# Norms between the layers: all tiles at once with scale and shift per feature, or tile by tile with a row scale and a shift added in PSUM

## Chip, cores, metric

One core of a Trainium2 chip runs the whole program in one launch. The metric is the device time of one execution in microseconds (us); the numbers are the median of three runs.

## The reference, cut to what matters

Two blocks of two layers each over 512 tokens of width 1024. The first block is a gated linear attention layer (GLA) and a dilated attention layer, each with memory attention; the second has a joint attention layer with a mixture of experts, then a neighbourhood attention layer with a second mixture. Each layer reads a normed residual:

```python
def rmsnorm(x, w):
    return (x * lax.rsqrt(jnp.mean(x * x, axis=-1, keepdims=True) + EPS)) * w
def modulate(x, g, shift, scale):
    return rmsnorm_2(x, g) * (1 + scale) + shift
# first block
for i in range(2):
    h = rmsnorm(x, norm_w[i])
    branch = mixer_i(h)                       # GLA, then dilated; gated
    x = x + branch @ w_out[i]
x = rmsnorm(x, final_norm_w)
# second block
for l in range(2):
    h_l = modulate(x_lat, norm_mix[l], sh1, sc1)
    h_c = modulate(x_ctx, norm_mix[l], sh1c, sc1c)
    o_c, o_l = mixer_l(h_c, h_l)              # joint attention, then neighbourhood
    x_lat = x_lat + g1 * o_l
    ...                                       # mixture of experts, adds to x_lat (and x_ctx)
```

Shift and scale are vectors over the 1024 features, computed in the program from the conditioning input.

## The kernel before, in words

The 512 tokens stand as four tiles of 128 rows x 1024 features (`K.tok`, tile `xres`); a layer's products want them with features on the partitions, as eight blocks of 128 features x 512 tokens, split into a high and a low part (`hh`, `hl`) whose three products make one float32 product (`mm3`, L256: lines 259 to 261).

**The norm.** `norm_T` (L367) takes all tiles of a set: it scales each by its reciprocal root (L377 on VectorE for odd tiles, L379 on ScalarE for even ones), transposes every 128x128 block on TensorE (L386) into one bank per feature block, and evacuates the bank. Without a shift, ScalarE writes the high part with the feature's scale (L390) and VectorE the low part (L391). With a shift, scale and shift go into a tile `nt` first, on ScalarE or VectorE in turn, and `split` (L137) makes the high part by a copy on ScalarE (L139) and the low part by a subtraction (L140), on VectorE or, for blocks 1 and 3, on GpSimd.

**Three places.** (G) The end of `gla_layer`, L793 to L808, before the dilated layer: no shift, and `phase_order` reorders tokens. (D) The end of `dil_layer`, L1100 to L1137, before the joint layer: latent norm with shift, composed with the first block's final norm (row `fw`), beside a norm of two context tiles. (N) `na_norms` (L2327), after the first mixture: the latent norm `lat()`, then `ctx()`, which adds the mixture to the two context tiles (`add_ctx`, L2194) and norms them.

**Order.** At G and D the norm is woven with the output product (`out_steps`, L683). `weave` (L24) advances several generators by estimated cost and due time (`yield cost, delay`); it sets the order in which each engine's instructions are written, and each engine runs its own in order. The output product makes 1024 columns in four parts of 256: two by `tm`, the last two together by `tm2` (L307), which finishes token tile after tile. `Residual.add` (L822) adds each part to the residual and collects sums of squares; `complete(tiles)` lets the norm go on. Before the change the norm asks for all four tiles. Between the product's own work VectorE and ScalarE also split the next weights (`cut`, L188: L208 and L211) and VectorE sums the conditioning product (L1396).

At N, `run(lat)` writes the whole latent norm first; then `weave(ctx, bg=(proj,))` writes the context part beside the next layer's projection, whose first context tile waits for the flag `nactx`. In `add_ctx` small placeholder DMAs on the SP queue (L2199, L2202) read `after`, which is `K.scaled`, a corner of the last scaled tile of the norm before; the rows are then fetched and added.

`features` (L355) brings vectors of 1024 into columns by a DMA each and one transpose. `na_mod` (L2316) does this for N; it is called inside `moe_layer` (L2294), between the routing table and the loop over overflow blocks.

Of the kernel before, what the change touches and what calls it, by code (L numbers as in the profile page):

```python
# [8 lines left out]
F32 = mybir.dt.float32  # L9
# [64 lines left out]
class Core:  # L74
# [289 lines left out]
        self.nc.vector.tensor_copy(t, ps[:, :n])  # L364
        return t

    def norm_T(self, pool, rows, rstd, hi, lo, sc, sh=None, tag="t", dst=None, src=lambda x: x):  # L367


        nc = self.nc  # L370
        n = len(rows)
        w = n * 128
        ys = []
        for i, x in enumerate(rows):
            y = pool.tile([128, D], F32, name=f"y{i}")
            if i % 2:
                nc.vector.tensor_scalar(y, x, rstd[i], None, op0=OP.mult)  # L377
            else:
                nc.scalar.activation(y, x, AF.Copy, scale=rstd[i])  # L379
            ys.append(y)  # L380
        self.scaled = ys[-1][0:1, 0:1]
        yield 0, 1500
        for k in range(8):
            ps = self.ps(tag)
            for i, y in enumerate(ys):
                nc.tensor.transpose(ps[:, i * 128:(i + 1) * 128], y[:, k * 128:(k + 1) * 128], self.ident)  # L386
            h, l = (dst(x[:, k, :]) if dst else x[:, k, :w] for x in (hi, lo))
            s = sc[:, k:k + 1]
            if sh is None:
                nc.scalar.activation(h, src(ps[:, :w]), AF.Copy, scale=s)  # L390
                nc.vector.scalar_tensor_tensor(l, src(ps[:, :w]), s, h.bitcast(F32), op0=OP.mult, op1=OP.subtract)  # L391
            else:
                t = pool.tile([128, w], F32, name="nt", bufs=3)
                if k % 2:
                    nc.scalar.activation(t, ps[:, :w], AF.Identity, scale=s, bias=sh[:, k:k + 1])
                else:
                    nc.vector.tensor_scalar(t, ps[:, :w], s, sh[:, k:k + 1], op0=OP.mult, op1=OP.add)
                self.split(h, l, src(t), nc.gpsimd if k in (1, 3) else None)
            yield n * 109, 0

    def bcast_row(self, pool, name, src, n=D, eng=None, **kw):

# [288 lines left out]
def gla_layer(K, A):  # L691
# [101 lines left out]
    K.dhh = ph.tile([128, 8, T], F32R, name="dhh")  # L793
    K.dhl = ph.tile([128, 8, T], F32R, name="dhl")
    with K.pool("gE", side="right") as st:
        nw = K.features(st, "nw1", [A["norm_w1"].rearrange("o (k p) -> (o k) p", p=128)])
        for i in range(4):
            nc.gpsimd.dma_start(xr[:, i, :], xin[i])
        r = Residual(K, st, K.tok, "gla", spill=[K.xbuf[i] for i in range(4)])

        def norms():
            yield from r.complete(range(4))
            rs = K.rsqrt(r.sum(range(4)), 4, 1.0 / D)
            yield 0, 2500
            yield from K.norm_T(st, K.tok, [rs[:, i:i + 1] for i in range(4)], K.dhh, K.dhl, nw,
                                dst=phases, src=phase_order)
        weave(norms(), out_steps(K, range(4), tokens(bh, bl), r.add))
    K.close(gC)  # L808
    K.close(gA)
# [223 lines left out]
def dil_layer(K, A):  # L1033
# [64 lines left out]
    with K.pool("dE") as st:  # L1098
        for i in range(4):
            nc.gpsimd.dma_start(xr[:, i, :], K.xbuf[i])  # L1100
        K.psum(p=(2, 512), t=(4, 512))
        fw = K.bcast_row(st, "fw", A["final_norm_w"], eng=nc.sync)
        r = Residual(K, st, K.tok, "dil", row=fw)
        vec = lambda ap: ap.rearrange("(k p) -> k p", p=128)
        m = K.features(st, "mv", [vec(K.mods[0, s, o * D:(o + 1) * D]) for s in range(2) for o in range(2)]
                       + [vec(A["norm_mix_2"][0]), vec(A["final_norm_w"])])
        sh, sc = [m[:, 0:8], m[:, 16:24]], [m[:, 8:16], m[:, 24:32]]
        for s in range(2):
            nc.vector.scalar_tensor_tensor(sc[s], sc[s], 1.0, m[:, 32:40], op0=OP.add, op1=OP.mult)
        nc.vector.tensor_tensor(sc[0], sc[0], m[:, 40:48], op=OP.mult)  # L1110
        tok = lambda k, tt: tuple(x[:, tt * 128:(tt + 1) * 128] for x in blocks(k))

        def ctx_norm():
            x = []
            for i in range(2):
                x.append(st.tile([128, D], F32, name=f"cx{i}"))
                nc.sync.dma_start(x[i], A["ctx_2"][i * 128:(i + 1) * 128, :])

            rs = K.row_rstd(x, K.hc[0].rearrange("p a b -> p (a b)")[:, :D])
            yield 0, 3000  # L1120
            yield from K.norm_T(st, x, [rs[:, i:i + 1] for i in range(2)], *K.hc, sc[1], sh[1])

        def norms():

            yield from r.complete(range(4))
            s1, s2 = r.sum(range(4)), r.sum(range(4), r.sw)
            u = K.small.tile([128, 4], F32, name="u")
            nc.vector.tensor_scalar(u, s1, EPS, EPS * EPS * D, op0=OP.mult, op1=OP.add)
            nc.vector.tensor_tensor(u, u, s2, op=OP.add)
            rs = K.rsqrt(u, 4, 1.0 / D, 0.0)  # L1130
            yield 0, 2500
            if K.stop != "b1":
                yield from K.norm_T(st, K.tok, [rs[:, i:i + 1] for i in range(4)], hh, hl, sc[0], sh[0])
            rs = K.rsqrt(s1, 4, 1.0 / D)
            for t in range(4):
                nc.vector.scalar_tensor_tensor(K.tok[t], K.tok[t], rs[:, t:t + 1], fw, op0=OP.mult, op1=OP.mult)
        weave(ctx_norm(), norms(), out_steps(K, range(4), tok, r.add))  # L1137
# [1175 lines left out]

def na_mod(K, A, p):  # L2316

    vec = lambda ap: ap.rearrange("(k p) -> k p", p=128)
    m = K.features(p, "mv", [vec(K.mods[1, s, o * D:(o + 1) * D]) for s in range(2) for o in range(2)]
                   + [vec(A["norm_mix_2"][1])], "h")  # L2320
    sh, sc = [m[:, 0:8], m[:, 16:24]], [m[:, 8:16], m[:, 24:32]]
    for s in range(2):
        K.nc.vector.scalar_tensor_tensor(sc[s], sc[s], 1.0, m[:, 32:40], op0=OP.add, op1=OP.mult)
    return sh, sc


def na_norms(K, hh, hl, p, cx, ss, mod):  # L2327


    nc = K.nc  # L2330
    sh, sc = mod

    def lat():
        rs = K.rsqrt(ss[:, 0:4], 4, 1.0 / D)
        yield from K.norm_T(p, K.tok, [rs[:, i:i + 1] for i in range(4)], hh, hl, sc[0], sh[0],
                            dst=lambda x: x[:, 64:576].rearrange("p (c r) -> p r c", r=8),
                            src=lambda t: t.rearrange("p (r c) -> p r c", c=64))
        nc.scalar.activation(hh[:, :, 0:64], hh[:, :, 512:576].bitcast(F32), AF.Copy)
        nc.scalar.activation(hl[:, :, 0:64], hl[:, :, 512:576].bitcast(F32), AF.Copy)

    def ctx():
        K.moe.add_ctx(p, cx, ss, K.scaled)
        yield 0, 9000
        rs = K.rsqrt(ss[:, 4:6], 2, 1.0 / D)
        yield from K.norm_T(p, cx, [rs[:, i:i + 1] for i in range(2)], hh[:, :, 576:], hl[:, :, 576:], sc[1], sh[1])
        K.set("nactx")
    return lat(), ctx()

# [151 lines left out]
def tile_two_blocks(ctx: ExitStack, tc: tile.TileContext, A, out, stop=None):  # L2500
# [27 lines left out]
    cx = [x2[:, i, :] for i in range(2)]  # L2528
    ss = p.tile([128, 6], F32, name="ss")
    mod = []  # L2530
    moe_layer(K, K.moe, K.tok, ss, lambda: mod.append(na_mod(K, A, p)))
    if stop == "moe0":
        return store()

# [146 lines left out]
```

## Time and profile before

| | |
|---|---|
| median of three runs | 3170.08 us (3168.34 to 3170.78) |
| the profiled execution's own time | 3168.85 us |
| its span, first to last instruction | 3167.1 us |
| mean granted TensorE clock | 0.961 |
| busy: PE / PEld / DVE / ACT / POOL | 92 / 77 / 72 / 57 / 18 % of the span |
| chain that ended last, by engine | PE 18 %, DVE 1 % |

PE is TensorE's products, PEld its weight loads (beside them), DVE VectorE, ACT ScalarE, POOL GpSimd, SP the queue that issues most transfers. A timeline row gives start, duration, engine, line, operation, output<-inputs and tile shape; in square brackets stands how long the engine idled before it and what ended that. A window row gives the busy time of each engine with its number of instructions, then the clock and the DMA share.

### The profile page before, as it was taken

What the parts mean: (1) busy time and instruction counts of PE and PEld (TensorE: products, weight loads), DVE (VectorE), ACT (ScalarE), POOL (GpSimd) and SP (SyncE); (2) the same over time, 40 slices, a digit from 0 to 9 for tenths busy, and PEclk for the clock granted to TensorE, in tenths of its full rate; (3) what the DMA queues carried; (4) which work ended last, traced back from release to release, by engine and by line L of the source; (5) the groups of instructions that cost most, each with busy time, mean ns of one, the idle gap of its engine ahead of it and who ended that gap; (6) DMA issues with size and microseconds to landing.
All of it is one profiled execution on the core that took longest, in us unless ns stands there. A gap on an engine that the chain in (4) does not pass through costs nothing. (4 is left out here: it accounts for less than half of the span.)

```text
span 3167.1 us, 46620 instructions
## 1 busy us (share of the span) xinstructions
PE 2906.3 (92%) x17395; PEld 2429.5 (77%) x17395; DVE 2264.8 (72%) x3684; ACT 1792.8 (57%) x2961; POOL 568.2 (18%) x871
## 2 busy tenths in 40 slices
PE   7989899999889889996999999959998789999997
PEld 6858688888779777785888888748887678888885
DVE  4776666765556566657898898875545688888888
ACT  4543534343352466534888788854334368878885
POOL 2110142523232111022111111020001211111110
PEclk9989999999989899997999999979999889999998
DMA  6334433433431200034999999954334399999996
GB/s 210 127 114 135 146 120 121 147 134 133 154 122 29 77 28 1 1 110 173 364 378 372 342 362 365 354 171 142 101 100 143 116 327 366 352 332 348 355 365 202
DMA packets 146089, 636.31 MB, mean 201 GB/s; under 512 B 30787, under 2 KB 37283, under 8 KB 86850
## 3 DMA queue, kind: packets, MB, share of 16 engines
q1 hardware_dynamic: 104034, 568.56, 49.6%
q0 software_dynamic: 29664, 50.29, 5.0%
q10 hardware_dynamic: 12160, 14.43, 1.9%
q8 instruction: 139, 2.28, 0.3%
q14 instruction: 92, 0.75, 0.1%
HBM read 615.13 MB, written 48.58 MB: 210 GB/s over the span
## 5 line engine op out<-in xcount | busy, mean ns | idle before, releaser
L211 DVE TENSOR_TENSOR wlo<-wraw,whi 128x1024 fp32r<-128x1024 f32 (+1 forms) x936 | 1105.6, 1222 | 251.4 <-ACT whi L208 239.2
L208 ACT ACTIVATE whi<-wraw 128x1024 fp32r<-128x1024 f32 (+1 forms) x938 | 935.9, 1051 | 184.7 <-PE ps_p L260 54.2
L260 PE MATMUL ps_h<-wlo,xth 128*128 128x512 f32 x1024 | 416.1, 406 | 1.3 <-DVE wlo L211 1.1
L259 PE MATMUL ps_h<-whi,xth 128*128 128x512 f32 x1024 | 409.5, 400 | 2.9 <-ACT xth L139 2.9
L261 PE MATMUL ps_h<-whi,xtl 128*128 128x512 f32 x1024 | 405.2, 396 | 0.0
L259 PE MATMUL ps_p<-whi,dhh 128*128 128x256 f32 (+3 forms) x828 | 248.5, 301 | 10.4 <-ACT qa L1541 6.4
L260 PE MATMUL ps_p<-wlo,dhh 128*128 128x256 f32 (+3 forms) x828 | 240.5, 291 | 0.0
L261 PE MATMUL ps_p<-whi,dhl 128*128 128x256 f32 (+3 forms) x828 | 239.5, 290 | 0.0
L259 PEld LDWEIGHTS ps_h<-whi,xth 128*128 128x128 f32 x1024 | 194.1, 190 | 48.3 <-ACT xth L139 4.0
L260 PEld LDWEIGHTS ps_h<-wlo,xth 128*128 128x128 f32 x1024 | 194.0, 189 | 47.5 <-DVE wlo L211 6.3
L261 PEld LDWEIGHTS ps_h<-whi,xtl 128*128 128x128 f32 x1024 | 193.7, 189 | 40.1
L259 PE MATMUL ps_y<-whi,hth 128*128 128x512 f32 x512 | 205.5, 401 | 5.8 <-DVE xg L2156 2.9
L1396 DVE SCALAR_TENSOR_TENSOR acc<-wraw,cs,acc 128x512 f32<-128x512 f32 x280 | 203.2, 759 | 9.7 <-DMA wraw<-in_w_ada_dram 8.1
L260 PE MATMUL ps_y<-wlo,hth 128*128 128x512 f32 x512 | 203.2, 397 | 0.2
L261 PE MATMUL ps_y<-whi,htl 128*128 128x512 f32 x512 | 202.5, 395 | 0.0
L2213 POOL DMA_INDIRECT xg<-hbuf,idx x64 | 86.5, 1351 | 545.3 <-PE ps_x L2224 480.8
L259 PEld LDWEIGHTS ps_p<-whi,dhh 128*128 128x128 f32 x828 | 157.7, 191 | 25.5 <-ACT qa L1541 6.6
L260 PEld LDWEIGHTS ps_p<-wlo,dhh 128*128 128x128 f32 x828 | 158.1, 191 | 1.3
L261 PEld LDWEIGHTS ps_p<-whi,dhl 128*128 128x128 f32 x828 | 157.7, 191 | 1.3
L2290 POOL DMA_INDIRECT ybuf<-y,idx x62 | 66.1, 1067 | 469.3 <-ACT y L2286 434.8
L139 ACT ACTIVATE xth<-ps_x 128x512 fp32r<-128x512 f32 x128 | 75.5, 590 | 76.4 <-PE ps_h L260 40.8
L259 PEld LDWEIGHTS ps_y<-whi,hth 128*128 128x128 f32 x512 | 96.7, 189 | 27.9 <-ACT whi L208 3.3
(792 smaller groups left out, 6716.4 us busy)
## 6 DMA issues: line engine op xcount, KB each, us to landing
wraw<-in_moe_w_gate_dram SPq DMA_DIRECT2D x128, 1024.0 KB
wraw<-in_moe_w_up_dram SPq DMA_DIRECT2D x128, 1024.0 KB
wraw<-in_moe_w_down_dram SPq DMA_DIRECT2D x128, 1024.0 KB
wraw<-in_w_ada_dram SPq DMA_DIRECT2D x48, 1024.0 KB
wraw<-in_db_w_dram SPq DMA_DIRECT2D x27, 1024.0 KB
wraw<-in_w_out_dram SPq DMA_DIRECT2D x8, 1024.0 KB
wraw<-in_na_qk_dram SPq DMA_DIRECT2D x8, 1024.0 KB
ntab<-in_na_tab_dram SPq DMA_DIRECT2D x16, 384.0 KB
```

Source lines behind the costliest of these rows:

```text
L139: nc.scalar.activation(hi, src, AF.Copy)
L208: self.nc.scalar.activation(h, x, AF.Copy)
L211: (self.cut_eng or self.nc.vector).tensor_tensor(l, x, h.bitcast(F32), op=OP.subtract)
L259: mm(out, ah, bh, start=first, stop=False)
L260: mm(out, ah, bl, start=False, stop=False)
L261: mm(out, al, bh, start=False, stop=last)
L1396: nc.vector.scalar_tensor_tensor(acc[s], x, w, acc[s], op0=OP.mult, op1=OP.add)
L2213: self.K.nc.gpsimd.indirect_dma_start(out=xg, out_offset=None, in_=self.hbuf, in_offset=bass.IndirectOffsetOnAxis(ap=gi, axis=0), bounds_c ...
L2290: self.K.nc.gpsimd.indirect_dma_start(out=self.ybuf, out_offset=bass.IndirectOffsetOnAxis(ap=si, axis=0), in_=y, in_offset=None, bounds_ch ...
```

## The change

`norm_tile` takes one tile: one VectorE instruction scales by the reciprocal root and by a broadcast row of feature scales; four blocks of 128 features go through TensorE into one bank of 512 columns (a transpose, or, with a shift, a float32 product with the identity and a one-row product of the shift with ones, which adds the shift in PSUM); ScalarE copies the bank and VectorE subtracts. At G and D tiles 0 and 1 are normed once `complete((0, 1))` holds, then 2, then 3; at N all four in a row. The scaled tiles take turns in two buffers `yt`. `scale_row` and `shift_row` fetch the rows; the latent vectors leave `features`.

```diff
--- before.py
+++ after.py
@@ -364,7 +364,7 @@
 
-    def norm_T(self, pool, rows, rstd, hi, lo, sc, sh=None, tag="t", dst=None, src=lambda x: x):
+    def norm_T(self, pool, rows, rstd, hi, lo, sc, sh=None, tag="t", dst=None, src=lambda x: x, ring=False):
 
@@ -372,7 +372,7 @@
         for i, x in enumerate(rows):
-            y = pool.tile([128, D], F32, name=f"y{i}")
+            y = pool.tile([128, D], F32, name="yt", bufs=2) if ring else pool.tile([128, D], F32, name=f"y{i}")
             if i % 2:
@@ -397,6 +397,47 @@
             yield n * 109, 0
+    def norm_tile(self, pool, x, rstd, row, shift, put, view=lambda v: v, tag="t"):
+        nc = self.nc
+        y = pool.tile([128, D], F32, name="yt", bufs=2)
+        nc.vector.scalar_tensor_tensor(y, x, rstd, row, op0=OP.mult, op1=OP.mult)
+        self.scaled = y[0:1, 0:1]
+        yield 0, 1500
+        for b in range(2):
+            ps = self.ps(tag)
+            for j in range(4):
+                k = slice((4 * b + j) * 128, (4 * b + j + 1) * 128)
+                o = ps[:, j * 128:(j + 1) * 128]
+                if shift is None:
+                    nc.tensor.transpose(o, y[:, k], self.ident)
+                else:
+                    nc.tensor.matmul(o, y[:, k], self.ident, start=True, stop=False)
+                    nc.tensor.matmul(o, shift[0][:, k], shift[1], start=False, stop=True)
+            h, l = put(b)
+            v = view(ps.rearrange("p (k t) -> p k t", k=4))
+            nc.scalar.activation(h, v, AF.Copy)
+            nc.vector.tensor_tensor(l, v, h.bitcast(F32), op=OP.subtract)
+            yield 870, 0
+    def scale_row(self, pool, l, side, w, t=None):
+        sc = pool.tile([128, D], F32, name="scrow")
+        if t is None:
+            t = pool.tile([128, D], F32, name="yt", bufs=2)
+        self.bcast(t, w)
+        self.bcast(sc, self.mods[l, side, D:2 * D])
+        self.nc.vector.scalar_tensor_tensor(sc, sc, 1.0, t, op0=OP.add, op1=OP.mult)
+        return sc
+    def shift_row(self, pool, l, side):
+        sh, one = pool.tile([1, D], F32, name="shrow"), pool.tile([1, 128], F32, name="one")
+        self.nc.gpsimd.memset(one, 1.0)
+        self.nc.sync.dma_start(sh, self.mods[l, side, 0:D].rearrange("(o n) -> o n", o=1))
+        return sh, one
 
@@ -793,17 +834,22 @@
     with K.pool("gE", side="right") as st:
-        nw = K.features(st, "nw1", [A["norm_w1"].rearrange("o (k p) -> (o k) p", p=128)])
+        nw = K.bcast_row(st, "nw1", A["norm_w1"], eng=nc.sync)
         for i in range(4):
         def norms():
-            yield from r.complete(range(4))
-            rs = K.rsqrt(r.sum(range(4)), 4, 1.0 / D)
-            yield 0, 2500
-            yield from K.norm_T(st, K.tok, [rs[:, i:i + 1] for i in range(4)], K.dhh, K.dhl, nw,
-                                dst=phases, src=phase_order)
+            for tts in ((0, 1), (2,), (3,)):
+                yield from r.complete(tts)
+                rs = K.rsqrt(r.sum(tts), len(tts), 1.0 / D)
+                yield 0, 2500
+                for i, t in enumerate(tts):
+                    put = lambda b: [x[:, 4 * b:4 * b + 4].rearrange("p k (r l) -> p k r l", r=4)[:, :, :, 32 * t:32 * t + 32]
+                                     for x in (K.dhh, K.dhl)]
+                    yield from K.norm_tile(st, K.tok[t], rs[:, i:i + 1], nw, None, put,
+                                           lambda v: v.rearrange("p k (l r) -> p k r l", r=4))
         weave(norms(), out_steps(K, range(4), tokens(bh, bl), r.add))
@@ -1102,12 +1148,12 @@
         vec = lambda ap: ap.rearrange("(k p) -> k p", p=128)
-        m = K.features(st, "mv", [vec(K.mods[0, s, o * D:(o + 1) * D]) for s in range(2) for o in range(2)]
-                       + [vec(A["norm_mix_2"][0]), vec(A["final_norm_w"])])
-        sh, sc = [m[:, 0:8], m[:, 16:24]], [m[:, 8:16], m[:, 24:32]]
-        for s in range(2):
-            nc.vector.scalar_tensor_tensor(sc[s], sc[s], 1.0, m[:, 32:40], op0=OP.add, op1=OP.mult)
-        nc.vector.tensor_tensor(sc[0], sc[0], m[:, 40:48], op=OP.mult)
+        m = K.features(st, "mv", [vec(K.mods[0, 1, o * D:(o + 1) * D]) for o in range(2)]
+                       + [vec(A["norm_mix_2"][0])])
+        sh, sc = m[:, 0:8], m[:, 8:16]
+        nc.vector.scalar_tensor_tensor(sc, sc, 1.0, m[:, 16:24], op0=OP.add, op1=OP.mult)
+        row, shift = K.scale_row(st, 0, 0, A["norm_mix_2"][0]), K.shift_row(st, 0, 0)
+        nc.vector.tensor_tensor(row, row, fw, op=OP.mult)
         tok = lambda k, tt: tuple(x[:, tt * 128:(tt + 1) * 128] for x in blocks(k))
@@ -1118,19 +1164,22 @@
             yield 0, 3000
-            yield from K.norm_T(st, x, [rs[:, i:i + 1] for i in range(2)], *K.hc, sc[1], sh[1])
+            yield from K.norm_T(st, x, [rs[:, i:i + 1] for i in range(2)], *K.hc, sc, sh, ring=True)
 
 
-            yield from r.complete(range(4))
-            s1, s2 = r.sum(range(4)), r.sum(range(4), r.sw)
-            u = K.small.tile([128, 4], F32, name="u")
-            nc.vector.tensor_scalar(u, s1, EPS, EPS * EPS * D, op0=OP.mult, op1=OP.add)
-            nc.vector.tensor_tensor(u, u, s2, op=OP.add)
-            rs = K.rsqrt(u, 4, 1.0 / D, 0.0)
-            yield 0, 2500
-            if K.stop != "b1":
-                yield from K.norm_T(st, K.tok, [rs[:, i:i + 1] for i in range(4)], hh, hl, sc[0], sh[0])
+            for tts in ((0, 1), (2,), (3,)):
+                yield from r.complete(tts)
+                n = len(tts)
+                u = K.small.tile([128, n], F32, name=f"u{n}")
+                nc.vector.tensor_scalar(u, r.sum(tts), EPS, EPS * EPS * D, op0=OP.mult, op1=OP.add)
+                nc.vector.tensor_tensor(u, u, r.sum(tts, r.sw), op=OP.add)
+                rs = K.rsqrt(u, n, 1.0 / D, 0.0)
+                yield 0, 2500
+                for i, t in enumerate(tts):
+                    put = lambda b: [x[:, 4 * b:4 * b + 4, t * 128:(t + 1) * 128] for x in (hh, hl)]
+                    yield from K.norm_tile(st, K.tok[t], rs[:, i:i + 1], row, shift, put)
+            s1 = r.sum(range(4))
             rs = K.rsqrt(s1, 4, 1.0 / D)
@@ -2313,28 +2362,31 @@
 
-def na_mod(K, A, p):
+def na_mod(K, A, p, t):
 
     vec = lambda ap: ap.rearrange("(k p) -> k p", p=128)
-    m = K.features(p, "mv", [vec(K.mods[1, s, o * D:(o + 1) * D]) for s in range(2) for o in range(2)]
+    m = K.features(p, "mv", [vec(K.mods[1, 1, o * D:(o + 1) * D]) for o in range(2)]
                    + [vec(A["norm_mix_2"][1])], "h")
-    sh, sc = [m[:, 0:8], m[:, 16:24]], [m[:, 8:16], m[:, 24:32]]
-    for s in range(2):
-        K.nc.vector.scalar_tensor_tensor(sc[s], sc[s], 1.0, m[:, 32:40], op0=OP.add, op1=OP.mult)
-    return sh, sc
+    sh, sc = m[:, 0:8], m[:, 8:16]
+    K.nc.vector.scalar_tensor_tensor(sc, sc, 1.0, m[:, 16:24], op0=OP.add, op1=OP.mult)
+    return sh, sc, K.scale_row(p, 1, 0, A["norm_mix_2"][1], t)
 
     nc = K.nc
-    sh, sc = mod
+    sh, sc, row = mod
+    shift = K.shift_row(p, 1, 0)
 
         rs = K.rsqrt(ss[:, 0:4], 4, 1.0 / D)
-        yield from K.norm_T(p, K.tok, [rs[:, i:i + 1] for i in range(4)], hh, hl, sc[0], sh[0],
-                            dst=lambda x: x[:, 64:576].rearrange("p (c r) -> p r c", r=8),
-                            src=lambda t: t.rearrange("p (r c) -> p r c", c=64))
+        for t in range(4):
+            put = lambda b: [x[:, 4 * b:4 * b + 4, 64:576].rearrange("p k (c r) -> p k r c", r=8)[:, :, 2 * t:2 * t + 2]
+                             for x in (hh, hl)]
+            yield from K.norm_tile(p, K.tok[t], rs[:, t:t + 1], row, shift, put,
+                                   lambda v: v.rearrange("p k (r c) -> p k r c", c=64))
         nc.scalar.activation(hh[:, :, 0:64], hh[:, :, 512:576].bitcast(F32), AF.Copy)
@@ -2342,7 +2394,7 @@
         rs = K.rsqrt(ss[:, 4:6], 2, 1.0 / D)
-        yield from K.norm_T(p, cx, [rs[:, i:i + 1] for i in range(2)], hh[:, :, 576:], hl[:, :, 576:], sc[1], sh[1])
+        yield from K.norm_T(p, cx, [rs[:, i:i + 1] for i in range(2)], hh[:, :, 576:], hl[:, :, 576:], sc, sh, ring=True)
         K.set("nactx")
@@ -2528,7 +2580,7 @@
     mod = []
-    moe_layer(K, K.moe, K.tok, ss, lambda: mod.append(na_mod(K, A, p)))
+    moe_layer(K, K.moe, K.tok, ss, lambda: mod.append(na_mod(K, A, p, cx[0])))
     if stop == "moe0":
```

## Rows read from the trace of the kernel before

**Rows 1.** Windows, three stretches: length, busy us (instructions) by engine, clock, DMA share, GB/s

```profile
310.00:325.50 15.50, 13.95 (x113) 13.42 (x112) 10.30 (x17) 4.08 (x11) 2.59 (x5) 1.00 0.55 190
...
916.00:932.20 16.20, 15.69 (x128) 15.04 (x126) 4.52 (x7) 7.38 (x24) 3.69 (x5) 1.00 0.04 16
...
1459.50:1485.50 26.00, 4.21 (x40) 3.66 (x39) 21.90 (x72) 9.33 (x22) 2.33 (x2) 0.50 0.51 198
```

**Rows 2.** Timeline of TensorE round three gaps: start us, us, engine, line, operation, tiles

```profile
325.21 0.28 PE L261 MATMUL ps_p<-whi,bl 128*128 128x256 f32 x1
...
340.89 0.48 PE L259 MATMUL ps_p<-dhh,whi 128*128 128x512 f32 x1
...
931.94 0.28 PE L261 MATMUL ps_p<-whi,b 128*128 128x256 f32 x1
...
947.37 0.36 PE L259 MATMUL ps_p<-whi,hc 128*128 128x256 f32 x1
...
952.43 0.39 PE L259 MATMUL ps_p<-whi,hc 128*128 128x256 f32 x1 [1.47 <-ACT gqk L1452]
...
2101.87 0.39 PE L2190 MATMUL ps_h<-xtl,oh 128*128 128x512 f32 x1
...
2122.51 0.58 PE L259 MATMUL ps_p<-whi,nhh 128*128 128x256 f32 x1 [6.51 <-ACT nhh L2338]
...
2123.80 0.58 PE L261 MATMUL ps_p<-whi,nhl 128*128 128x256 f32 x1 [0.28 <-ACT nhl L2339]
```

**Rows 3.** Timeline: the scaling behind the reciprocal roots, at the three places

```profile
333.15 2.19 ACT L379 ACTIVATE y<-xres,ringdtfloat 128x1024 f32<-128x1024 f32 x2 [5.21 <-DVE ringdtfloat L343]
...
938.68 2.19 ACT L379 ACTIVATE y<-xres,ringdtfloat 128x1024 f32<-128x1024 f32 x2 [3.63 <-DVE ringdtfloat L343]
...
2106.64 1.42 DVE L377 TENSOR_SCALAR y<-xres,ringdtfloat 128x1024 f32<-128x1024 f32 x2
```

**Rows 4.** Groups by line and shape, VectorE and ScalarE: busy us, mean ns

```profile
L140 DVE TENSOR_TENSOR nhl<-nt,nhh 128x512 fp32r<-128x512 f32 x6 | 7.4, 1247 | 2.4 <-ACT nhh L139 2.4
...
L1878 DVE SCALAR_TENSOR_TENSOR H<-xres,ringdtfloat,sc 128x1024 f32<-128x1024 f32 x8 | 10.3, 1282 | 0.5
...
L391 DVE SCALAR_TENSOR_TENSOR dhl<-ps_t,nw,dhh 128x512 fp32r<-128x512 f32 x8 | 5.4, 740 | 0.0
...
L139 ACT ACTIVATE nhh<-nt 128x512 fp32r<-128x512 f32 x8 | 8.3, 1141 | 0.1
...
L390 ACT ACTIVATE dhh<-ps_t,nw 128x512 fp32r<-128x512 f32 x8 | 5.1, 689 | 1.4 <-PE ps_t L386 1.4
```

**Rows 5.** Timeline: four float32 products (two instructions each); weight loads of four transposes

```profile
113.90 1.08 PE L965 MATMUL ps_h<-xres 96*128 96x128 f32 x8
114.74 0.36 PE L259 MATMUL ps_p<-whi,hh 128*128 128x256 f32 x1
...
339.16 0.42 PEld L386 LDWEIGHTS ps_t<-ident,y 128*128 128x128 f32 x4 [0.24 <-DVE dhl L391]
```

**Rows 6.** Windows, TensorE alone: length, busy us (instructions), granted clock, DMA share, GB/s

```profile
936.00:945.00 9.00, 5.12 (x23) 0.50 0.39 134
946.00:951.00 5.00, 4.43 (x36) 1.00 0.01 3
...
2107.00:2113.00 6.00, 5.10 (x23) 0.50 0.32 126
...
2122.00:2126.00 4.00, 3.21 (x13) 0.50 0.89 171
```

**Rows 7.** Timeline: the context rows of the last norm, first DMA to transposes

```profile
2108.13 0.75 SPq L2199 DMA_DIRECT2D gc<-y  x1
...
2133.89 1.15 ACT L379 ACTIVATE y<-cx,ringdtfloat 128x1024 f32<-128x1024 f32 x1
...
2137.84 2.11 PE L386 MATMUL ps_t<-ident,y 128*128 128x128 f32 x14
```

**Rows 8.** Timeline of VectorE: its first instruction behind the routing table

```profile
1485.79 2.36 DVE L211 TENSOR_TENSOR wlo<-wraw,whi 128x1024 fp32r<-128x1024 f32 x2 [3.59 <-SPq L2078]
```

## The prediction, made before the changed kernel ran

> **What bounds the kernel now.** I read the page first: TensorE is busy 92 % of the span, so almost any time that the change gives or takes is time in which TensorE stands still or runs other instructions. TensorE's timeline at the three places comes next. At G it ends the output product at 325.49 us (325.21 + 0.28) and starts the next layer's first product at 340.89: a gap of 15.40 us that holds little but the norm. At D the gap runs from 932.22 to 947.37, 15.15 us, and a stall of 1.47 us follows at 952.43. At N it runs from 2102.26 to 2122.51, 20.25 us [rows 2]. The scaling starts at 333.15, 938.68 and 2106.64 [rows 3]: 7.66, 6.46 and 4.38 us after the last product, which is the sums' and roots' share; the rest is transposes and evacuation. Last, the windows: while the output product still runs VectorE is busy 10.30 of 15.5 us at G and 4.52 of 16.2 us at D [rows 1], so 5.2 and 11.7 us are free for work brought forward.
>
> **Prices.** A transpose takes TensorE 0.105 us (four in 0.42). A float32 product is two instructions, and eight of them take 0.84 us: 0.21 us a product [rows 5]. Scaling by root and row has the form of L1878: 1.28 us. The low and the high part of 512 columns take 0.74 and 0.69 us (L391, L390), at N, where the output is regrouped, 1.25 and 1.14 us (L140, L139) [rows 4].
>
> **The change part by part**, against the profiled execution's own 3168.85 us (span 3167.1 and 1.75 around it; the median of the runs is 1.2 above it).
>
> *G.* Tiles 0 and 1 are normed while tm2 works on tiles 2 and 3. Their 16 transposes come between products: 16 x 0.105 = +1.7 us on TensorE's path. Behind the last product tile 3 sets the end; tile 2 fits into the wait for tile 3's root. The chain: 7.66 us to the root, as before, since the same small instructions queue behind the same filler; scaling 1.28; 8 transposes 0.85; evacuation 0.69 + 0.74; hand-overs 0.3, an estimate: 11.5 us. So 1.7 + 11.5 = 13.2 against 15.4: −2.2. Against it, VectorE gets 2 x 1.28 + 4 x 0.74 = 5.5 us beside the product and a second chain of some dozen small instructions, which I put at 0.19 each (the present chain fits with its filler into 7.66 us, so one is under 0.6): 7.8 us into a free 5.2. The overrun of 2.6 delays the residual additions, which free the product's banks (0 if filler gives way, 7.8 if nothing fits). TensorE starts the next layer after fewer transposes, perhaps at a lower clock: +0.6 (0 to 2). G: +1.0, bounds −5.3 (root within 4 us, no overrun) to +7.
>
> *D.* Each block now costs two float32 products, with the identity and with the one-row shift: 16 x 0.21 = 3.4 us a tile, where transposes were 0.84. The one-row product isn't in the rows; the nearest has 96 rows, and I give it the same price (0, if a single row is nearly free, to 0.21, which makes 1.7 to 3.4 a tile). Tiles 0 and 1 put 6.7 us into the product, on the path; VectorE's 7.8 us there fit into 11.7. Behind the last product: root 6.46, scaling 1.28, hand-over 0.2, tile 3's products 3.4 at full clock or 6.7 at half; then TensorE goes on with the context projection (hc is its first operand there), which needs none of this norm. That is 6.7 + 11.3 = 18.0, or 21.4, against 15.15: +2.9 to +6.2. The 1.47 stall may go: +1.4 to +4.7. I take +3.0. That GpSimd no longer subtracts is worth nothing where VectorE has room.
>
> *The routing table of the first mixture.* na_mod gets one more 128x1024 VectorE instruction, 1.28 us [rows 4], and two transfers of 512 KB on SP's queue. That stage is VectorE's: 21.90 of 26 us, TensorE 4.21 [rows 1], and a weight split waits right behind, at 1485.79, itself 3.59 us idle for SP [rows 8]. +1.3 (0 if it slips into that wait, 3 if its rows come late).
>
> *N, the latent norm.* Tile 0 is scaled from 2106.64, so products start at 2107.95. While the clock is at half, as it was there up to 2113 [rows 6], 12 products run in 5.3 us; the other 52 take 10.9, and TensorE ends at 2124.2. ScalarE's last copy, 1.14, and the wrap copy (L2338; I take 0.63, its time being bounded by the 1.25 between 2122.51 and the wait's end for L2339 at 2123.80) bring the first projection to 2126.1 against 2122.51, and its low parts to 2127.4 against 2123.80 [rows 2]: +3.6. The projection began at half clock (2122 to 2126 [rows 6]) and would now start at full: −1.5. Together +2.1 (−1 to +6).
>
> *N, the context.* Placeholder DMAs on SP read K.scaled. Before, that was tile 3's scaled row, done at 2108.06 (2106.64 + 1.42), and SP issued the first at 2108.13 [rows 3, 7]. Now tiles share two buffers: tile 2's scaling waits for tile 0's products (2114.0), tile 3's for tile 1's (2117.4), so K.scaled is written at 2118.7, 10.6 us later. Queued behind it: SP's fetches, GpSimd's gathers, VectorE's multiply and add, and the scaling that now ends at 2135.04 (2133.89 + 1.15); the transposes start at 2137.84 [rows 7], so 2.8 us of the 10.6 are slack. They would start at 2145.6: +7.8, which takes in the latent +2.1, since the projection of the four latent tiles just ends earlier and TensorE waits from 2139.9 for the context's flag. Bounds for N as a whole +2.1 (the wait filled or the fetches quicker) and +10 (the clock falls in it). I take +7.
>
> A row and a rule: TensorE's clock is at half in 936 to 945, while the norm's transposes are most of what it runs, and full in 946 to 951 [rows 6], so here it rose with transposes and the first projection products. The Trainium skill, page "TensorE: Matmul & The Clock Gate", section "Part 4: PE-mode transpose", says that full clock isn't engaged by transposes, since they don't count as busy in the same way. By it the real products of D and N would bring full clock where transposes couldn't, and the sum would be some 2 us lower.
>
> The sum: G 1.0 + D 3.0 + table 1.3 + N 7.0 = +12.3 on 3168.85, which is 3181.2; with the median's 1.2, some 3182 us.
>
> **The rivals.**
> 1. *The context's wait is hidden.* The scheduler puts other ready projection work into it, or the fetches are quicker; N is +2.1, and D at its low end: 1.0 + 1.4 + 1.3 + 2.1 = +5.8, 3176. For it: TensorE is rarely without work here (92 %). Against it: the projection's program order waits for the context's flag.
> 2. *Faster: the root comes early.* The chain behind the last product is the price at G and D, and filler stands in it: 7.66 and 6.46 us, where at N it takes 4.38 [rows 2, 3]. With one tile left instead of four the order may put less filler in front. At a root after 4 us G gives −5.3 without overrun, D −1.1 (6.7 + 3.9 + 1.3 + 0.2 + 3.4 − 15.15 − 1.47, rounded), N −1, the table 0: −7.4, 3162.6. It decides once the root is under some 4 us at both. Against it: the same VectorE serves both, and gets more to do.
> 3. *Worse: VectorE is late inside the product.* Nothing of the 7.8 us at G fits, the clock is at half for D's last tile, and N takes its +10: 7 + 4.7 + 1.3 + 10 = +23, 3193. For it: one in-order VectorE does evacuation, residual additions and splits. Against it: at D it has twice the room.
>
> **How the numbers follow.** The forecast gets 0.48, the hidden wait 0.24, the early root 0.13, late VectorE 0.15. The forecast's own range is 3176 to 3187. The range 3163 to 3193 leaves out the halves of the outer two and some of the surprises. A difference under 0.2 %, 6.3 us, can't be told from none: faster means under 3163.8, slower over 3176.4. Faster: the early root, 0.13. Within: most of the hidden wait and a low tail of the forecast, less what rounds out of it: 0.24. Slower: the rest, 0.63.
>
> **What would show it.** For G: 16 transposes of the norm before the last product, and a gap from there to dhh of about 11.5 us; with a longer wait of L827's additions the overrun is right. For D: 32 float32 products before the last output product and a gap of about 11 us; if a one-row product takes much under 0.21 us, D is too dear. For N: SP's first placeholder at about 2118 and TensorE idle before the context's transposes; if the placeholder comes within 3 us of the old time, or TensorE doesn't idle there, the largest term is wrong. The table's term shows as the first split behind it coming 1.3 us later. The whole is wrong if the gaps at G and D shrink by more than what the product grows.

## The result: 2.55 % slower, and the profile after

The changed kernel takes 3251.6 us (median of four runs, 3250.39 to 3253.04) against 3169.21 us before (the three runs above and one more): ratio 1.0255, 95 % interval 1.0241 to 1.0269. The sign was forecast, the size was not: +82 us instead of +12.

The page after: span and busy time by engine. TensorE's share is 92 % as before, but of a longer span: its busy time went from 2906.3 to 2997.6 us. The time is lost in work on TensorE, not in waits for it.

```profile
span 3249.8 us, 47044 instructions
...
PE 2997.6 (92%) x17586; PEld 2492.4 (77%) x17586; DVE 2283.3 (70%) x3744; ACT 1777.9 (55%) x2947; POOL 565.4 (17%) x869
```

Groups of TensorE by line and shape (busy us, mean ns). L417 is the identity product, L418 the one-row product; 128 instructions each are 64 products of each kind. At full clock they were forecast at 128 x 0.21 = 27 us, and they are busy 95.3.

```profile
L417 PE MATMUL ps_t<-ident,yt 128*128 128x128 f32 x128 | 47.7, 473 | 11.2 <-DVE yt L406 6.2 <-DVE ringdtfloat L343 5.0
L418 PE MATMUL ps_t<-one,shrow 1*128 1x128 f32 x128 | 47.6, 470 | 0.0
```

TensorE's timeline at D, which answers to [rows 2]. A product takes 0.40 us in the first rows (a pair from 932.38 to 933.18) and 0.72 soon after (936.35 to 937.07). The output product ends at 964.78 (before: 932.22), the context projection starts at 985.90 (before: 947.37): a gap of 21.1 us, where the prediction named about 11.

```profile
932.38 0.46 PE L417 MATMUL ps_t<-ident,yt 128*128 128x128 f32 x2 [0.49 <-DVE yt L406]
...
933.18 0.49 PE L417 MATMUL ps_t<-ident,yt 128*128 128x128 f32 x2
...
936.35 0.79 PE L418 MATMUL ps_t<-one,shrow 1*128 1x128 f32 x2
937.07 0.80 PE L417 MATMUL ps_t<-ident,yt 128*128 128x128 f32 x2
...
964.50 0.28 PE L261 MATMUL ps_p<-whi,b 128*128 128x256 f32 x1
...
985.90 0.58 PE L259 MATMUL ps_p<-whi,hc 128*128 128x256 f32 x1
```

At N: from the first product at 2155.32 to the last TensorE has no gap, and the projection starts 53.9 us after the last product of the mixture (before: 20.25).

```profile
2149.20 0.40 PE L2239 MATMUL ps_h<-xtl,oh 128*128 128x512 f32 x1
2155.32 0.80 PE L417 MATMUL ps_t<-ident,yt 128*128 128x128 f32 x2 [5.72 <-DVE yt L406]
...
2203.52 0.58 PE L259 MATMUL ps_p<-whi,nhh 128*128 128x256 f32 x1 [1.84 <-ACT nhh L2390]
```

Windows of TensorE alone (length, busy with instructions, granted clock), which answer to [rows 6]. The clock is full when tile 0's pairs begin and half from 936, though TensorE was busy throughout both; all 46.3 us at N are at half. There 128 instructions are 64 products: 0.72 us each.

```profile
932.30:935.60 3.30, 3.22 (x16) 1.00 0.00 0
936.00:941.40 5.40, 5.40 (x16) 0.50 0.00 0
...
2155.30:2201.60 46.30, 46.28 (x128) 0.50 0.29 82
```

To see where the 82 us are, I took every instruction that both kernels have and compared its start in the two profiled executions; the shift, grouped by stretch of the kernel before, only changes in a few places. Each column is what the shift gains between its two ends; one row for each kernel told of below. I call this the ledger.

```
stretch:     G        to D     D        joint    table    mixture  N         rest     sum
before us:   300-380  -860     -960     -1440    -1480    -2100    -2160     -3000
after        -3.5     +1.5     +41.1    +2.1     +3.5     +2.8     +35.2     +0.2     +82.9
row128       -3.5     +0.4     +12.4    +2.3     +3.4     +3.0     +10.4      0.0     +28.4
no_shift     -1.3     +0.5     +5.8     +4.3     +3.6     +1.2     +8.9      -1.8     +21.2
ctx_early    -4.0     +0.8     +6.2     +1.3     +3.4     +3.4     -0.6      -1.0     +9.5
late_rows    -3.6     +1.6     +1.6     +3.9     +3.6     +0.9     +8.7      -1.8     +14.9
repaired     -3.0     +0.6     +11.9    +2.1     +5.3     +2.5     +7.0      -0.7     +25.7
shift_pool   -4.3     +1.8     +17.2    +1.9     +3.9     +2.8     +2.5      -2.5     +23.3
g_only       -4.0     +0.8     +0.6     +3.4     +0.4     -0.2     +0.2      +1.2     +2.4
g_23         -5.5     +0.7     +0.7     +3.8     +2.4     +0.8     +0.3      -1.9     +1.3
```

These are single executions against the one profiled before, so a difference of 2 us in a column is not much, and where a column ends can move as much into its neighbour. The verdicts go by the ratios of the timed runs, each to runs of the kernel before made beside it, whose medians there were 3172.58 to 3173.23 us; by them the later kernels come out 1 to 7 us lower than the sums of their rows (g_23: 5.3 us faster, where its row says 1.3 slower).

### The profile page after: what moved, and what is told of

The parts are those of the page before. It is cut to its first block, busy times and chain, and to the rows that moved or that the text cites. A ratio compares the mean times of both kernels' runs of the same rounds, so it can differ in the third digit from the quotient of the medians.

```text
span 3249.8 us, 47044 instructions
## 1 busy us (share of the span) xinstructions
PE 2997.6 (92%) x17586; PEld 2492.4 (77%) x17586; DVE 2283.3 (70%) x3744; ACT 1777.9 (55%) x2947; POOL 565.4 (17%) x869
## 5 line engine op out<-in xcount | busy, mean ns | idle before, releaser
L139 ACT ACTIVATE xth<-ps_x 128x512 fp32r<-128x512 f32 x128 | 75.4, 589 | 76.5 <-PE ps_h L260 41.1
```

Of the source, the lines that this page charges most:

```text
L139: nc.scalar.activation(hi, src, AF.Copy)
```

## The experiments

**What does a float32 product cost, and what does it do to the clock?** Each stretch of `micro` begins with 70 dense products that bring the clock up, then repeats one form:

```
tr:        transpose(o, x[:, k], ident)                        # x 64
ident:     mm(o, x[:, k], ident)          # 128 rows             x 64
one_row:   mm(o, row[:, k], one)          # 1 row                x 64
full_row:  mm(o, row8[:, k], one8)        # 128 rows, 127 zero   x 64
rows96:    mm(o, x[:96, k], ident[:96])   # 96 rows              x 64
pair:      ident, then one_row accumulated on it                 x 48
pair_full: ident, then full_row accumulated on it                x 48
alone:     ident, one_row, each closed by itself                 x 48
```

> Leaves the whole model out: TensorE alone runs eight stretches, each a run of 70 dense fp32r products to bring the clock up and then 64 float32 instructions' worth of one kind: transposes; identity products (128 rows); one-row products; 128-row shift products; 96-row products; pairs identity + one-row accumulated as in the changed kernel; pairs identity + 128-row; pairs identity + one-row each closed by itself. Theory A (a lone row loses the clock): one-row stretches and the pairs with one row fall to 0.50 and cost 0.72 us a product there, identity, 128-row and 96-row stretches keep 1.00. Rival B (float32 products as such lose it): all but the transposes fall. On the price at full clock: theory P (0.42 us a product is what float32 costs, whatever is next to it) expects 0.42 for identity alone, rival Q (changing from 128 rows to one and back makes the load wait) expects 0.21 for identity alone and 128-row pairs, and 0.42 only for the mixed pairs.

Windows inside the stretches: transposes, identity, one-row before and after the clock fell, full_row, rows96, pair before and after it fell.

```profile
15.00:22.00 7.00, 7.00 (x66) 1.00 0.01 2
34.00:47.00 13.00, 13.00 (x119) 1.00 0.00 0
58.00:61.40 3.40, 3.40 (x31) 1.00 0.00 0
65.00:80.00 15.00, 15.00 (x72) 0.50 0.01 1
95.00:108.00 13.00, 13.00 (x119) 1.00 0.00 0
120.00:133.00 13.00, 13.00 (x119) 1.00 0.00 1
145.70:149.00 3.30, 3.30 (x18) 1.00 0.00 0
151.00:180.00 29.00, 29.00 (x81) 0.50 0.00 1
```

Two products of one pair at full clock:

```profile
146.38 0.49 PE L2600 MATMUL ps_p<-ident,y 128*128 128x128 f32 x2
146.80 0.48 PE L2601 MATMUL ps_p<-one,row 1*128 1x128 f32 x2
```

Transposes, identity, full_row and rows96 stay at full clock; 119 instructions in 13 us are 0.109 each, 0.22 us a product. One-row products cost the same 0.22 as long as the clock is full (31 instructions in 3.4 us), then it falls to half with TensorE never idle, and they cost 0.42 (72 in 15). The pairs lose the clock too, and besides cost more at either level: 0.42 a product at full (from one start to the next, 146.38 to 146.80), 0.72 at half (81 instructions in 29 us). The groups tell accumulation from the row count: products of pairs closed one by one (L2609) take as long as those of accumulated pairs (L2600), and those beside a 128-row partner (L2604) 275 ns an instruction, as transposes do.

```profile
L2609 PE MATMUL ps_p<-one,row 1*128 1x128 f32 x96 | 36.8, 482 | 0.0
...
L2600 PE MATMUL ps_p<-ident,y 128*128 128x128 f32 x96 | 36.2, 478 | 0.0
...
L2604 PE MATMUL ps_p<-ident,y 128*128 128x128 f32 x96 | 18.6, 275 | 0.0
```

So theory A and the price of rival Q hold together: products over a single row lose the clock, and where 128 rows and one take turns each product takes about another 0.2 us at full clock. That it is the weight load which waits, as Q has it, was not tested. Nor was any change of rows but that between 128 and one.

**The same in the kernel.** `row128` widens the shift's operands to 128 rows, the rest zeros:

```diff
-        sh, one = pool.tile([1, D], ...), pool.tile([1, 128], ...)
-        self.nc.gpsimd.memset(one, 1.0)
+        sh, one = pool.tile([128, D], ...), pool.tile([128, 128], ...)
+        self.nc.gpsimd.memset(one, 0.0)
+        self.nc.gpsimd.memset(one[0:1, :], 1.0)
+        self.nc.gpsimd.memset(sh, 0.0)
...
```

> The changed kernel with the one-row shift widened to 128 rows, 127 of them zeros; sums and results the same. Theory A (a lone row loses the clock): the clock stays at 1.00 in the norm's products, 0.42 or 0.21 us each, total 3195 to 3225. Rival B (any float32 product loses it): as the changed kernel, 3245 to 3255.

3197.73 us (one run): 54 us less than the changed kernel (58 if each is taken against the kernel before beside it), for shift products over 128 rows instead of one. The groups: 56.2 us instead of 95.3, and the ledger puts 28.7 us of the gain at D and 24.8 at N.

```profile
L417 PE MATMUL ps_t<-ident,yt 128*128 128x128 f32 x128 | 28.5, 309 | 13.4 <-DVE yt L406 6.9 <-DVE ringdtfloat L343 6.5
...
L418 PE MATMUL ps_t<-one,shrow 128*128 128x128 f32 x128 | 27.7, 302 | 0.0
```

**What is left without the shift.** `no_shift` leaves the latent shift out and transposes at all three places:

```diff
-                if shift is None:
+                if True:
                     nc.tensor.transpose(o, y[:, k], self.ident)
```

> The changed kernel with the latent shift left out: transposes at D and N too, all else as changed. If the float32 products are the cause (theory A or B): D loses some 30 us of its 41, N some 30 of its 35, total 3180 to 3195. If the waits are (broadcast rows on SP, K.scaled late, two buffers): over 3215.

3189.6 us, ratio 1.0050 (1.0033 to 1.0067): as expected, and still slower than before. In the ledger it keeps +5.8 at D, +3.6 at the table and +8.9 at N. At N, the last tile's scaling with what VectorE ran ahead of it, SP's first placeholder, and the context's transposes:

```profile
2126.26 5.01 DVE L422 TENSOR_TENSOR nhl<-ps_t,nhh 128x512 fp32r<-128x512 f32 x5
...
2131.16 1.30 DVE L406 SCALAR_TENSOR_TENSOR yt<-xres,ringdtfloat,scrow 128x1024 f32<-128x1024 f32 x1
...
2132.49 0.71 SPq L2248 DMA_DIRECT2D gc<-yt  x1
...
2159.29 3.88 PE L386 MATMUL ps_t<-ident,yt 128*128 128x128 f32 x16 [4.96 <-ACT yt L379]
```

The placeholder follows the scaling of the last tile; against the shift of some 14 us that the kernel has there, it is 10.4 us late (2132.49 - 2108.13 - 14.0; forecast 10.6), and the transposes 7.5 (2159.29 - 2137.84 - 14.0; forecast 7.8). That the sizes agree is partly luck: the forecast had tile 3's scaling wait for tile 1's products, but with transposes TensorE is done with tiles 0 and 1 at 2125.46, and the scaling stands behind five subtractions on VectorE instead.

**That wait taken away.** `ctx_early`, on no_shift, gives `add_ctx` a corner of the roots:

```diff
+        K.scaled = rs[0:1, 0:1]
         nc.scalar.activation(hh[:, :, 0:64], ...)
```

> As no_shift (the latent shift left out, transposes throughout), and K.scaled at N is a corner of the roots, ready before the first scaling, instead of the last tile's scaled row. If the context's wait for that row is the +8 us that no_shift still shows at N: SP's first placeholder comes some 10 us sooner, the context's transposes 6 to 8 sooner, ratio to before 1.0020 to 1.0030. If the wait is hidden by something else (the gathers, the roots of the context): ratio 1.0045 to 1.0055 as no_shift.

3178.46 us, ratio 1.0018 (1.0009 to 1.0028), just under the expected 1.0020 to 1.0030. N is -0.6 where no_shift had +8.9. The placeholder and the transposes:

```profile
2118.94 0.70 SPq L2248 DMA_DIRECT2D gc<-ringdtfloat  x1
...
2149.58 2.11 PE L386 MATMUL ps_t<-ident,yt 128*128 128x128 f32 x14
```

**The stall ahead of D.** In the changed kernel TensorE stands 5.47 us in the first part of D's output product: VectorE's residual addition waits 6.68 us for the residual's reload.

```profile
892.57 0.58 PE L259 MATMUL ps_p<-whi,b 128*128 128x256 f32 x1 [5.47 <-DVE xres L873]
...
891.76 0.75 DVE L873 TENSOR_TENSOR xres<-xres,ps_p 128x256 f32<-128x256 f32 x2 [6.68 <-DMA xres<-xbuf]
```

The same addition before:

```profile
888.73 0.75 DVE L827 TENSOR_TENSOR xres<-xres,ps_p 128x256 f32<-128x256 f32 x2 [1.53 <-DMA xres<-xbuf]
```

`late_rows`, on no_shift, moves the two broadcasts in program order to where the product's last tile has its first quarter:

```diff
-        row, shift = K.scale_row(...), K.shift_row(...)
-        nc.vector.tensor_tensor(row, row, fw, op=OP.mult)
...
         def norms():
+            yield K.has("dil", 3, 0)
+            row, shift = K.scale_row(...), K.shift_row(...)
+            nc.vector.tensor_tensor(row, row, fw, op=OP.mult)
```

> As no_shift, but the 512 KB broadcasts at D are issued when the output product's last tile has its first quarter, instead of ahead of it. If they hold up the reload of the residual (the 5 us stall at about 888 us): that stall goes back to under 2 us, ratio to before 1.003 to 1.0035. If the row then comes too late for tiles 0 and 1, the stall moves into the norm and the ratio is 1.005.

3183.43 us, ratio 1.0028 (1.0016 to 1.0040), and D is +1.6 instead of +5.8. The stall is nearly halved, not gone; the expectation of under 2 us missed. TensorE now stands 2.65 us (no_shift: 4.70), and VectorE's addition waits 3.87 (6.62):

```profile
889.14 0.75 DVE L873 TENSOR_TENSOR xres<-xres,ps_p 128x256 f32<-128x256 f32 x2 [3.87 <-DMA xres<-xbuf]
```

The SP queue of late_rows shows that the edit did only half of what it was meant to: one of the broadcasts came late. The other went out at 879.41, ahead of the product's part that stalls and about when no_shift issues it (879.50), only behind the context's reads.

```profile
879.41 0.33 SPq L449 DMA_DIRECT2D scrow<-mods  x1
...
903.68 0.33 SPq L449 DMA_DIRECT2D yt<-in_norm_mix_dram  x1
```

So the two were never late together, and how much of the stall each makes stays open; g_only, which has no broadcasts at D, has no wait of VectorE for that reload over 1 us.

**Do the terms add?** `repaired` is row128 with both edits.

> The changed kernel with three edits: 128-row shift (as row128), K.scaled from the roots, the rows at D late. By the ledger, row128's ratio of some 1.008 less 0.002 to 0.003 for the context and 0.0015 for the rows: 1.003 to 1.005, still slower than before, from float32 products at 0.44 us a block against 0.11 and the longer table. If the terms don't add, over 1.006.

3192.64 us, ratio 1.0058 (1.0043 to 1.0074): little better than row128, over what was expected. At D there was little to win: in row128 TensorE's stall was only 2.57 us, with both broadcasts early, and it is 1.60 here (+11.9 against +12.4). N falls from +10.4 to +7.0. There the context's work, now early, runs into the latent evacuation on ScalarE and VectorE: the first projection waits 6.20 us for ScalarE,

```profile
2150.22 0.58 PE L259 MATMUL ps_p<-whi,nhh 128*128 128x256 f32 x1 [6.20 <-ACT nhh L2394]
```

where in row128 it waited 1.84:

```profile
2144.98 0.38 PE L259 MATMUL ps_p<-whi,nhh 128*128 128x256 f32 x1 [1.84 <-ACT nhh L2392]
```

In ctx_early the norm's own chain is shorter, and the same edit was worth 9.5 (+8.9 to -0.6).

**The shift on another engine.** `shift_pool` adds it on GpSimd ahead of transposes, with both edits:

```diff
         nc.vector.scalar_tensor_tensor(y, x, rstd, row, op0=OP.mult, op1=OP.mult)
+        if shift is not None:
+            nc.gpsimd.tensor_tensor(y, y, shift, op=OP.add)
...
-                if shift is None:
-                    nc.tensor.transpose(o, y[:, k], self.ident)
-                else:
-                    ...
+                nc.tensor.transpose(o, y[:, k], self.ident)
```

> The whole change with the shift added elsewhere: GpSimd adds a 128-row broadcast of it to the scaled tile, and TensorE transposes at all three places; K.scaled from the roots, rows at D late. If the lone-row products are the whole difference between the idea and its cost, this is the sum of ctx_early and late_rows against no_shift (1.005 less 0.003 less 0.002: 1.000) plus what GpSimd's additions lay on the path, at 2.36 us a tile (L211's form on GpSimd): one tile at D and two to four at N, 2 to 10 us: ratio 1.0005 to 1.0035. Under 0.999 would say that norms tile by tile are worth having at D and N; over 1.0045 that the third broadcast or GpSimd costs more than the sum.

3195.04 us, ratio 1.0069 (1.0048 to 1.0089), a miss. N is only +2.5, but D +17.2. GpSimd there also multiplies for the second sum (L836 before), in order with the additions, and its additions for tiles 2 and 3 wait for VectorE's scaling, which stands behind the sums and roots. They begin 5.0 and 13.3 us after the output product's end (946.46), where the scaling before started after 6.46. Besides, TensorE's stall in the product is back, at 5.06 us: two of the three broadcasts went out at 880.96 and 881.34.

```profile
951.48 3.31 POOL L408 TENSOR_TENSOR yt<-yt,shrow 128x1024 f32<-128x1024 f32 x1 [2.96 <-DVE ringdtfloat L894]
959.78 2.34 POOL L408 TENSOR_TENSOR yt<-yt,shrow 128x1024 f32<-128x1024 f32 x1 [5.00 <-DVE ringdtfloat L342]
```

**G alone.** `g_only` has the change at G and nowhere else.

> The change at G alone; D, N and na_mod as before. If the time is lost at D and N by the float32 products, as the ledger of the trace says, this is 3164 to 3172 us, ratio 0.998 to 1.001. If the new order at G (scaling in one VectorE instruction, two buffers) is itself a cost, over 3175.

3169.39 us, ratio 0.9992 (0.9982 to 1.0002): no change that can be told. The last scaling behind the last product (which ends at 326.70) and the next layer's first product:

```profile
338.32 1.28 DVE L406 SCALAR_TENSOR_TENSOR yt<-xres,ringdtfloat,nw 128x1024 f32<-128x1024 f32 x1
...
341.52 0.79 PE L259 MATMUL ps_p<-dhh,whi 128*128 128x512 f32 x1
```

`g_23` norms tiles 2 and 3 together: `for tts in ((0, 1), (2, 3))`.

> The change at G alone, with tiles 2 and 3 normed together after the last product: one chain of roots instead of two, so less filler between its steps. In g_only the last scaling came 11.6 us after the last product, before 7.7. If the two chains are what lengthens it, the scaling comes at 7 to 9 us, ratio 0.9975 to 0.9990; if not, 0.9985 to 1.0005.

3167.95 us, ratio 0.9981 (0.9972 to 0.9990): faster than the kernel before by 0.19 %. Against g_only it can't be told: the intervals overlap. The scaling of both starts 8.2 us after the last product (326.78), and the next layer 13.1 us after it, where g_only had 14.8:

```profile
334.95 2.48 DVE L406 SCALAR_TENSOR_TENSOR yt<-xres,ringdtfloat,nw 128x1024 f32<-128x1024 f32 x2
...
339.85 0.79 PE L259 MATMUL ps_p<-dhh,whi 128*128 128x512 f32 x1
```

## Why the prediction was wrong, point by point

**The step that failed** is the price of the one-row product at D and N: "the nearest has 96 rows, and I give it the same price (0, if a single row is nearly free, to 0.21, ...". The range was open on the wrong side. By itself one row does cost 0.22 us at full clock (`micro`), so the nearest row was right for the instruction; missing were two effects that go beyond the instruction: where the row count changes, every product takes 0.42 instead of 0.22, its identity partner too, and the clock falls, which makes it 0.72. Of the 82.9 us in the ledger these are 53.5 (changed kernel against row128). For the clock I let full follow from dense work ("the projection ... would now start at full"); at N it was half throughout, 46.3 us for 64 products against 16.2 forecast (5.3 + 10.9).

**D** was +41.1 against +3.0. From the ledger of row128 and no_shift: 28.7 us are the lone row, 6.6 what products at 128 rows cost over transposes (12.4 - 5.8), where the prices of the prediction give some 7.6 for the three tiles that it has on the path (3.4 - 0.84 each); 4.2 go with moving the broadcasts (no_shift against late_rows): about 2 are the shorter stall, about 2 the clock, which no_shift has at half from 890.5 to 897.3 and late_rows at full. The broadcasts I had not priced at D at all, only their issue at the table; in the trace of before the residual's reload already kept VectorE waiting 1.53 us.

**N** was +35.2 against +7.0. 24.8 us are the lone row. The context's wait is confirmed in its place where TensorE's part is short (no_shift +8.9, gone in ctx_early). row128, whose products come nearest to the price, has the placeholder 11.7 us late (2137.70 - 2108.13 - 17.9) and N at +10.4, a little over the bound of 10. In the changed kernel the wait is hidden behind 46 us of products: the placeholder is 23.7 us late (2179.17 - 2108.13 - 47.3), but TensorE idles only 1.16 us before the context's transposes, so there the largest term of the sum was not what made N late.

```profile
2219.68 1.97 PE L386 MATMUL ps_t<-ident,yt 128*128 128x128 f32 x14 [1.16 <-ACT yt L379]
```

**The table** was +3.5 against +1.3, over its upper bound of 3: the added scaling runs 1.23 us and waits another 1.07 for its broadcast, inside the table's chain on VectorE. The other 1.2 us were not traced.

```profile
1511.34 1.23 DVE L432 SCALAR_TENSOR_TENSOR scrow<-scrow,cx 128x1024 f32<-128x1024 f32 x1 [1.07 <-DMA scrow<-mods]
...
1530.31 2.36 DVE L211 TENSOR_TENSOR wlo<-wraw,whi 128x1024 fp32r<-128x1024 f32 x2 [3.84 <-SPq L2127]
```

The first split behind it waits 3.84 for SP as it did 3.59 before, so what is late ahead of it is not made up in that wait.

**G** was -3.5 against +1.0; the eight kernels with the same G gave -1.3 to -4.3. The gap itself:

```profile
326.27 0.28 PE L261 MATMUL ps_p<-whi,bl 128*128 128x256 f32 x1
...
338.18 1.29 DVE L406 SCALAR_TENSOR_TENSOR yt<-xres,ringdtfloat,nw 128x1024 f32<-128x1024 f32 x1
...
340.92 0.50 PE L259 MATMUL ps_p<-dhh,whi 128*128 128x512 f32 x1 [0.25 <-ACT dhh L421]
```

From 326.55 to 340.92 it is 14.4 us, not 11.5: the last scaling came 11.6 us after the product instead of 7.66, because two chains of small instructions, each with filler between its steps, replace one; `g_23` shows that. The product's end came 1.1 us later, not 1.7 plus an overrun of 2.6. Together that leaves the next layer's first product where it was (340.92 against 340.89). Half clock up to 345.3 and a wait of 0.64 us for VectorE then make it +2.4, where I had +0.6 (0 to 2) for a lower clock. Then some 6 us come back at 354 to 366 us, where VectorE before stood 4.79 us for a conditioning chunk and TensorE 4.64 for ScalarE behind it; in the nine kernels with the change at G TensorE's wait there is 2.25 us at most, in the changed one none. What brings the chunk sooner was not tried.

**What the ledger adds between the places.** In g_only the -4.0 after G is +0.8 by 1440, and every kernel here shows such losses (the columns "to D" and "joint"). The clock falls to half around small gaps at which it held before: in g_only 0.79 in 556 to 564 us and 0.69 in 1221 to 1231, against 1.00 in both stretches before. But this doesn't show that the change costs it. The one execution of before in the ledger had a granted clock of 0.961, while 23 later ones had 0.956 to 0.962, with 0.958 in the middle, and took 3177 to 3178 us at the lowest clock and 3164.70 at the highest; and the timed runs leave g_only 3.6 us under the kernel before, where its row has +2.4. Whether these falls come with the change or with the execution stays open.

**The rule weighed.** The prediction took from the Trainium skill, page "TensorE: Matmul & The Clock Gate", section "Part 4: PE-mode transpose", that transposes don't engage full clock, and so that real products would lift it where transposes can't. Here 64 transposes in a row held 1.00 (`micro`), and before the change it rose to 1.00 in the midst of the transposes at N, with nothing else on TensorE since 5.64 us of idling. Real products over one row lost it: the measurement decides.

```profile
2107.90 5.94 PE L386 MATMUL ps_t<-ident,y 128*128 128x128 f32 x28 [5.64 <-ACT y L379]
...
2113.00:2115.00 2.00, 0.84 (x7) 0.95 0.93 281
```

The same page of the Trainium skill, section "Why this matters for your kernels", says that a single product over 32 rows takes the time of one over 128. No run here has 32 rows; 1, 96 and 128 rows in `micro` agree at full clock (0.22 us each). That is the price of the instruction alone, and it misled.

Two ends of the prediction's range at G don't follow from its own terms, without effect here: no gain left and the whole overrun make +7.6, not +7 (-2.2 + 7.8 + 2), and an early root with no cost of the clock makes -5.9, not -5.3. Of the rivals none came. The third (VectorE late inside the product) had the right sign and the price nearest, for another reason.

## What to carry to other kernels

A one-row product to add a vector in PSUM costs what one over 128 rows does only while the clock holds and no 128-row products alternate with it: between those it nearly doubled their time and the clock fell to half, and padding its operands with zeros to 128 rows took 54 us off this kernel. When the nearest row for a new operation differs from it in shape, leave the upper end of its price open, and ask what it does to its neighbours. Before work is split into tiles, count the serial chains that it multiplies (roots, sums) and the filler that an in-order engine puts between their steps: at G the next layer began 13.1 us after the last product with one chain for two tiles, 14.8 with two.

## What the runs showed of the hardware

- A float32 product of 128 columns was two instructions and 0.22 us at full clock whether it summed 1, 96 or 128 rows.
- Where products over 128 rows and over one row took turns, each took about 0.2 us more at full clock (0.42 instead of 0.22), accumulated or not.
- TensorE's clock fell to 0.50 in the midst of unbroken one-row products and of pairs with one row, and stayed there as long as nothing else ran; with 128 rows, 127 of them zeros, it stayed at 1.00. Under transposes alone it rose from 0.50 to 1.00 (before the change, at N).
- With two 512 KB broadcasts on SP's queue ahead of it, the wait for a reload issued by GpSimd was 6.68 us instead of 1.53 (4.76 in row128); with one of the two issued only after it, it was 3.87.
